# The product of C and the state in three parts, B and C loaded by chunk, and another order in layer 1

## The chip, the cores and the metric

The kernel runs on one core of one Trainium2 chip. The metric is the device time of one execution in microseconds. Three runs of the kernel before took 1805.58, 1814.24 and 1804.48 us; the median is 1805.58 us. TensorE (PE) multiplies, VectorE (DVE), ScalarE (ACT) and GpSimd (POOL) do the elementwise work, and SyncE (SP) issues most transfers. PEld in the profile is TensorE's weight load.

## The reference

Two layers over 1024 latent and 256 context tokens of width 1024, all in float32. Layer 0 has a gated linear recurrence beside a differential attention; the change doesn't touch it. Layer 1 is a Mamba-2 mixer in both directions, with 32 heads of 64 in 4 groups that share B and C. It is computed in chunks of 128 tokens:

```python
z, xbc, dt = jnp.split(u @ w_in, [SSD_INNER, SSD_INNER + SSD_CONV_DIM], axis=-1)
xbc = jax.nn.silu(dwconv_centred(xbc, conv_w, conv_b))
xs, Bm, Cm = jnp.split(xbc, ...)
...
CB = jnp.einsum("bclgn,bcsgn->bcgls", Cc, Bc)
y_diag = jnp.einsum("bcgls,bgrcls,bcsgrp->bclgrp", CB, Lmat, Xc)
states = jnp.einsum("bclgn,bgrcl,bclgrp->bcgrpn", Bc, decay_states, Xc)
...
y_off = jnp.einsum("bclgn,bcgrpn,bgrcl->bclgrp", Cc, states_in, jnp.exp(A_cs))
...
y = ys[0] + ys[1] + d_skip * xs          # both directions
y = rms_norm(y * silu(z), norm_w) @ w_out  # norm per group, then the output projection
```

The product `Cc` with `states_in` in `y_off` is the one that the change computes in another way.

## The kernel before, in words

Layer 1 runs from about 830 to 1812 us of the profile. It has four stages.

- The dt stage (`dt_block`, 830 to 911 us) makes the step sizes and their sums, and turns three tables (`wd`, `ea`, `dtt`) with TensorE transposes. It stores `d_acs`, `d_ncs` and `d_et` in HBM.
- The blocks of B, C and x (`conv_block`, 911 to 1240 us). Each group has one block of B, one of C and four of x. A block is a projection of 128 columns over all tokens (L303, from `proj`), four convolution taps on DVE (L329, L331) and an activation on ACT (L712). A projection is made as three float32r products: weight and input are each split in a high part and a rest, and high x high, rest x high and high x rest are summed. ACT casts the high part of the weights (L282), DVE subtracts for the rest (L283). The x blocks are then transposed to token order (L723), scaled on POOL (L744, `x2w`), split (L752 on ACT, L753 on POOL) and stored in `d_x`. B is split likewise (`bkh`, `bkl`) and stored in `d_bk`; B and C also go to `d_bt` and `d_ct`, whole.
- The z blocks (`z_block`, 16 of them; nz, which is 3, come before the B and C blocks, the rest at 1240 to 1410 us). Between them go the first steps of the states of group 0: `k.step` takes x2 from `d_x` (L908) and `bk` (L887) and multiplies them (L929).
- The chunk stage (`ssd`, 1410 to 1812 us): 4 groups of 8 chunks. `front(s)` makes the masks (L1050, L1052, L1053, L1055), CB (L1034) and the product of C with the states of both directions (L1061, one float32 matmul each), which DVE and POOL scale and add (L1064, L1067, L1069). `mid(s)` transposes that sum into psdy (L1078), adds the product within the chunk (L1083), and gates and splits it. `back(s)` is the output projection (L1119) and the sum over groups in `acc` (L1129); in the last group it also makes the final norm (L1134, L1143). `front` runs two steps ahead of `back`, `mid` one. `r_g` and `r_y` are the reciprocal roots that the two norms need, made on POOL (L218).

Inside each engine instructions run in order. A scheduler writes that order from its own model of the program when the kernel is built, so a line that is moved in the source moves in the engines' rows as far as the scheduler lets it. Pools are regions of on-chip memory: a pool that is opened where another was closed waits for what was using the space.

## Time and profile before

| what | us |
|---|---|
| median of three runs | 1805.58 |
| the profiled execution | 1813.9 |
| its span (first to last instruction) | 1812.1 |
| TensorE busy in the span | 1728.8 (95%) |
| VectorE busy | 1130.6 (62%) |
| ScalarE busy | 820.4 (45%) |
| GpSimd busy | 484.8 (27%) |

The chain of work that ended last is 71% TensorE, 9% DVE, 6% DMA, 5% POOL, 4% ACT. So the kernel is mostly as long as its matmuls, and the rest is in places where TensorE stands. The granted clock of TensorE (PEclk) is a share of its full speed; 0.50 is the lower of its two levels.

How to read rows of the trace: a row of the timeline has a start, a length, the engine, the line, the operation and what it writes and reads; in brackets is the idle time before it and what ended it. xN at the end means N instructions in a row. Matmuls are pipelined: a row's length has overlap with its neighbours in it, so the distance of two starts tells what a matmul takes.

### The profile page before, as it was taken

Reading aid. Unit: us, or ns where it says so; the run is one execution under the profiler, and the core shown is the slowest. Engines: PE = TensorE matmul, PEld = TensorE weight load, DVE = VectorE, ACT = ScalarE, POOL = GpSimd, SP = SyncE. Lnnn points to the kernel's source line nnn. Section 1 sums busy time; section 2 is a strip of 40 time slices with the busy share of each in tenths; the row PEclk is TensorE's granted clock in tenths of the full one; section 3 lists DMA queues with packets and bytes.
Section 4 is the critical chain, followed back from the end, with each engine's and each line's share of the span. In section 5 each row is a group of like instructions: output and inputs, shape, how many; then the busy total and the mean of one; then the engine's idle time right before and its main releaser. Section 6 shows DMA issues by size and latency. Waiting matters only on the chain.

```text
span 1812.1 us, 24291 instructions
## 1 busy us (share of the span) xinstructions
PE 1728.8 (95%) x8946; PEld 1343.8 (74%) x8946; DVE 1130.6 (62%) x1646; ACT 820.4 (45%) x1607; POOL 484.8 (27%) x459
## 2 busy tenths in 40 slices
PE   5999999999999998999999999998899899999997
PEld 2765478888888877886778888887678577777775
DVE  4635566766748476666666666665121667878787
ACT  5552464565536465544344443435111555434443
POOL 1200210000000000110029494948010344444432
PEclk8999999999999999999899999999899999999999
DMA  8336532622231224433238584858843677777764
GB/s 270 121 96 191 156 105 94 168 60 76 79 108 65 71 94 148 135 124 92 68 122 217 166 225 152 227 161 242 286 148 102 205 247 270 252 258 252 248 229 146
DMA packets 264637, 293.45 MB, mean 162 GB/s; under 512 B 16393, under 2 KB 213006, under 8 KB 264006
## 3 DMA queue, kind: packets, MB, share of 16 engines
q1 hardware_dynamic: 236336, 262.73, 46.3%
q10 hardware_dynamic: 28182, 29.16, 4.9%
q8 instruction: 71, 1.16, 0.3%
q14 instruction: 48, 0.39, 0.1%
HBM read 187.49 MB, written 100.42 MB: 159 GB/s over the span
## 4 chain that ended last, share of the span: by engine, by line
PE 71%; DVE 9%; DMA 6%; POOL 5%; ACT 4%; issue 4%; ACTq 0%; SPq 0%; DVEq 0%; POOLq 0%
PE psap L303 19%; PE pscp L303 10%; PE psap L1119 7%; PE psbp L303 7%; PE pscp L1427 3%; PE psat L591 3%; PE psat L929 2%; PE psdo L1061 2%; PE psap L1427 2%; PE scores L539 2%; PE psat L587 1%; PE scores L540 1%; PE psdy L1083 1%; POOL x2w L744 1%; DMA wm<-in_w_mod_dram 1%
## 5 line engine op out<-in xcount | busy, mean ns | idle before, releaser
L331 DVE SCALAR_TENSOR_TENSOR xbc<-xp_xb,pb,xbc 128x1283 f32<-128x1283 f32 (+1 forms) x72 | 141.7, 1972 | 2.9
L744 POOL TENSOR_TENSOR x2w<-tok_x,wd 128x1152 f32<-128x1152 f32 (+2 forms) x48 | 118.2, 2488 | 47.3 <-ACT tok_x L724 47.3
L940 POOL TENSOR_TENSOR s<-s,etb 128x512 f32<-128x512 f32 x64 | 70.9, 1107 | 205.0 <-DVE s L941 96.7
L602 POOL TENSOR_TENSOR ors<-z,mhalf 128x4 f32<-128x4 f32 (+1 forms) x12 | 14.5, 1212 | 380.4 <-DVE z L600 313.8
L941 DVE TENSOR_TENSOR s<-s,psat 128x512 f32<-128x512 f32 x64 | 43.6, 681 | 100.0 <-PE psat L929 76.5
L753 POOL TENSOR_TENSOR x2l<-x2w,x2h 128x1152 fp32r<-128x1152 f32 x32 | 104.4, 3282 | 0.1
L1119 PE MATMUL psap<-wo1h,yh 128*128 128x512 f32 x256 | 102.4, 400 | 0.0
L1119 PE MATMUL psap<-wo1h,yl 128*128 128x512 f32 x256 | 100.9, 395 | 1.5 <-DVE yl L1090 1.5
L1119 PE MATMUL psap<-wo1l,yh 128*128 128x512 f32 x256 | 101.1, 395 | 0.0
L329 DVE TENSOR_SCALAR xbc<-xp_xb,pb 128x1283 f32<-128x1283 f32 (+1 forms) x24 | 31.1, 1294 | 108.2 <-ACT xp_xb L321 86.3
L303 PE MATMUL pscp<-u1H,wh_xb 128*128 128x512 f32 x232 | 93.5, 403 | 0.0
L303 PE MATMUL pscp<-u1H,wl_xb 128*128 128x512 f32 x232 | 93.3, 402 | 0.0
L303 PE MATMUL pscp<-u1L,wh_xb 128*128 128x512 f32 x232 | 93.2, 402 | 0.0
L303 PE MATMUL psap<-u1H,wl_z 128*128 128x512 f32 x224 | 89.3, 399 | 0.0
L303 PE MATMUL psap<-u1H,wh_z 128*128 128x512 f32 x224 | 89.2, 398 | 0.0
L303 PE MATMUL psap<-u1L,wh_z 128*128 128x512 f32 x224 | 89.1, 398 | 0.0
L564 ACT ACTIVATE p<-scores,nm 128x1024 f32<-128x1024 f32 x64 | 71.5, 1118 | 28.4 <-DVE nm L563 20.8
L929 PE MATMUL psat<-x,bk 128*128 128x512 f32 x216 | 75.5, 457 | 7.8 <-DMA x<-d_x 7.8
L539 PE MATMUL scores<-kk,xq 128*128 128x512 f32 (+1 forms) x208 | 77.2, 383 | 3.7 <-ACT p L564 2.7
L752 ACT CAST x2h<-x2w 128x1152 fp32r<-128x1152 f32 x32 | 37.2, 1161 | 88.1 <-POOL x2w L744 88.1
L540 PE MATMUL scores<-kk,xl 128*128 128x512 f32 (+1 forms) x208 | 72.7, 361 | 0.0
L591 PE MATMUL psat<-v,wT 128*128 128x128 f32 x572 | 71.3, 278 | 0.0
(479 smaller groups left out, 5083.1 us busy)
## 6 DMA issues: line engine op xcount, KB each, us to landing
...
```

Of the source, the lines that this page charges most:

```text
L303: nc.tensor.matmul(ps[:n, :w_], l[:, k, :], r[:, k, t0 : t0 + w_], start=(k == 0 and i == 0), stop=(k == KT - 1 and i == 2))
L331: nc.vector.scalar_tensor_tensor(out[:, j0 : j0 + n], xp[:, j0 + k : j0 + k + n], cw(k), out[:, j0 : j0 + n], OP.mult, OP.add)
L539: nc.tensor.matmul(out, xq[m][:, qs], kk[m][:, k0 : k0 + n], start=True, stop=False)
L540: nc.tensor.matmul(out, xl[:, m, qs], kk[m][:, k0 : k0 + n], start=False, stop=True)
L564: nc.scalar.activation(pr[m][:, NCTX:], scores[m], AF.Exp, bias=nm[:, m : m + 1], accum_out=zz[:, 1, m : m + 1])
L591: nc.tensor.matmul(po[:, :P], wT[:, j, :], v[:, j, :], start=(j == 0), stop=(j == nkt - 1))
L744: nc.gpsimd.tensor_tensor(x2[:, o : o + n, :].rearrange("p c (h e) -> p c h e", e=64), t[:, a0:a1, :].rearrange("p c (h e) -> p c h e", e=64),
L753: nc.gpsimd.tensor_tensor(l, x2, h.bitcast(F32), OP.subtract)
L929: nc.tensor.matmul(ps, bk[:, l, t, :], x2[:, r, :], start=(i == 0), stop=(i == 2))
L940: nc.gpsimd.tensor_tensor(sn, self.prev[g, d], self.et[:, hs, t : t + 1].to_broadcast([P, 8, 64]), OP.mult)
L1119: nc.tensor.matmul(po, l[:, q, :], w[:, n], start=(q == 0 and i == 0), stop=(q == 3 and i == 2))
L1427: nc.tensor.matmul(ps, l[:, k, :], r[:, k, n], start=(k == 0 and i == 0), stop=(k == KT - 1 and i == 2))
```

## The change

Part (a), the order of layer 1: the pool p1 is opened before the dt stage's own pool instead of after it, and a new pool p1s holds the split tiles; the transposes of the three tables are put in a function `turn`, called after z block 0; z block 3 is computed before the last x block is finished (before, only its weights were fetched there); the group's loads and the first two x2 loads come before z block 4. The transfers of `et` go from ACT's queue to SP's. Part (b): C and each state are split in a high part and a rest, and C times the state is three float32r products. C's parts are made once for each group and stored in `d_cs`, the state's parts are made by `state_parts`, with ACT's cast and POOL's subtraction, in tiles of one buffer. Part (c): B and C in float32, and C's parts, are stored by chunk and loaded by chunk. Part (d): the multiplication `yg` of the last group is on POOL, but for the last chunk. The tiles `cb` and `td` have one buffer instead of two.

```diff
-    nc.scalar.dma_start(dr["et"], tot)
+    nc.sync.dma_start(dr["et"], tot)
...
+    def turn():
+        for src, dst in ((rm, wd), (acs, ea), (dt, dtt)):
+            for j0, n in ((0, 8), (8, 2)):
+                ps = c.psum()
+                for j in range(n):
+                    nc.tensor.transpose(ps[:, j * 64 : (j + 1) * 64], src[:, (j0 + j) * P : (j0 + j + 1) * P], c.ident[:64, :64])
+                pv = ps[:, : n * 64].rearrange("p (j h) -> p j h", h=64)
+                if dst is dtt:
+                    o = 2 if j0 == 0 else 0
+                    nc.vector.tensor_copy(dtt[:, j0 + o - 2 : j0 + n - 2, :], pv[:, o:n, 32:64])
+                else:
+                    nc.vector.tensor_copy(dst[:, j0 : j0 + n, :], pv)
+
+    return (wd, ea, et, dtt), turn
...
+        pool = s1.enter_context(tc.tile_pool(name="p1", bufs=2, side="right"))
         with tc.tile_pool(name="dtp", bufs=1, side="right") as dp:
-            tabs = dt_block(c, a, xdt, dp, scst, dr)
-        pool = s1.enter_context(tc.tile_pool(name="p1", bufs=2, side="right"))
-        for i in range(nz):
+            tabs, turn = dt_block(c, a, xdt, dp, scst, dr)
+            z_block(c, a, 0, uH, uL, zp, dr)
+            turn()
+        spool = s1.enter_context(tc.tile_pool(name="p1s", bufs=2, side="right"))
...
+        def by_chunk(e, dst, src):
+            e.dma_start(dst.rearrange("c p l -> p c l"), src.rearrange("p (c l) -> p c l", l=P))
...
-                nc.scalar.dma_start(dr["ct"][g], xc[:, 259:XC])
+                by_chunk(nc.scalar, dr["bc"][g, :, :, 1, :], xc[:, 259:XC])
+                h, l = (spool.tile([P, NLAT], F32R, name=f"ct{m}{g}", tag=f"ct{m}", bufs=1) for m in "hl")
+                nc.scalar.copy(h, xc[:, 259:XC])
+                nc.gpsimd.tensor_tensor(l, xc[:, 259:XC], h.bitcast(F32), OP.subtract)
+                store.append(lambda: [by_chunk(nc.sync, dr["cs"][g, :, :, m, :], x.bitcast(F32)) for m, x in enumerate((h, l))])
...
-        prefetch(c, a["o_w_in"][0][:, nz * P : (nz + 1) * P], f"z{nz}")
+        z_block(c, a, nz, uH, uL, zp, dr)
...
-    for i in range(nz, 16):
+    k.group(0)
+    for n in range(2):
+        k.step_x(0, "p", n)
+    for i in range(nz + 1, 16):
         z_block(c, a, i, uH, uL, zp, dr)
         if i == EARLY:
             early, rest = ssd(c, a, k, dr, S, out, h_d)
             early()
-        if i == nz:
-            k.group(0)
-            k.load_bc(0)
-            for n in range(3):
-                k.step_x(0, "p", n) if n < 2 else None
-        else:
-            n = i - nz - 1
-            if n < 9:
-                k.step(0, "p", n)
-                if n + 2 < 9:
-                    k.step_x(0, "p", n + 2)
-            if n >= 9 or n in (6, 7):
-                k.step(0, "j", {6: 0, 7: 1, 9: 2}.get(n, 2)) if n in (6, 7, 9) else None
+        n = i - nz - 2
+        if 0 <= n < 9:
+            k.step(0, "p", n)
+            if n + 2 < 9:
+                k.step_x(0, "p", n + 2)
+        if n in (6, 7, 9):
+            k.step(0, "j", {6: 0, 7: 1, 9: 2}[n])
...
+    def state_parts(s):
+        g, it = divmod(s, NCH)
+        ch = chunk_of(g, it)
+        out = []
+        for d in range(2):
+            st = k.st[g, d, ch].rearrange("p h e -> p (h e)")
+            h, l = (p1.tile([P, 512], F32R, name=f"s{m}{g}_{ch}{d}", tag=f"s{m}{d}", bufs=1) for m in "hl")
+            nc.scalar.copy(h, st)
+            nc.gpsimd.tensor_tensor(l, st, h.bitcast(F32), OP.subtract)
+            out.append((h, l))
+        sts[s] = out
...
+        bc = p1.tile([P, 2, P], F32, name=f"bc{nm}", tag="bc")
+        nc.sync.dma_start(bc, dr["bc"][g, ch])
+        cs = p1.tile([P, 2, P], F32R, name=f"cs{nm}", tag="cs")
+        nc.sync.dma_start(cs.bitcast(F32), dr["cs"][g, ch])
...
-        cb = p1.tile([P, 1, P], F32, name=f"cb{nm}", tag="cb")
+        nc.tensor.matmul(pcb[:, :P], bc[:, 0, :], bc[:, 1, :], start=True, stop=True)
+        cb = p1.tile([P, 1, P], F32, name=f"cb{nm}", tag="cb", bufs=1)
...
-            nc.tensor.matmul(py, ct[:, l0 : l0 + P], k.st[g, d, ch].rearrange("p h e -> p (h e)"), start=True, stop=True)
+            sh, sl = sts[s][d]
+            for i, (l, r) in enumerate(((0, sh), (1, sh), (0, sl))):
+                nc.tensor.matmul(py, cs[:, l, :], r, start=(i == 0), stop=(i == 2))
...
-                nc.vector.tensor_tensor(y, acc[:, n], gp[:, n], OP.mult)
+                e = nc.vector if s == N - 1 else nc.gpsimd
+                e.tensor_tensor(y, acc[:, n], gp[:, n], OP.mult)
...
+            if 2 <= s + 2 < N:
+                state_parts(s + 2)
```

TensorE in a chunk of the first groups, around the product of C (`ct` or `cs`) with a state (`s`, or its parts `sh` and `sl`) into `psdo`; before:

```order
L1034 MATMUL psda_12280<-ct_10543,bt_10541 128x128
L1050 MATMUL psda_12298<-At_10463,Rt_10466 128x512
L1061 MATMUL psdo_12314<-s_10683,ct_10543 128x512
L1050 MATMUL psda_12300<-At_10463,Rt_10466 128x512
L1061 MATMUL psdo_12318<-s_12058,ct_10543 128x512
L929 MATMUL psat_12324<-x_12247,bk_11540 128x512 x3
L1119 MATMUL psap_12345<-wo1h_11518,yh_2_12131 128x512
L1119 MATMUL psap_12345<-wo1l_11519,yh_2_12131 128x512
L1050 MATMUL psda_12306<-At_10463,Rt_10466 128x512
```

and of the change:

```order
L1049 MATMUL psda_12575<-bc_0_12569 128x128
L1065 MATMUL psda_12593<-At_10540,Rt_10543 128x512
L931 MATMUL psat_12636<-x_12532,bk_12526 128x512
L1065 MATMUL psda_12595<-At_10540,Rt_10543 128x512
L1078 MATMUL psdo_12609<-sh_00_12534,cs_0_12571 128x512 x2
L1078 MATMUL psdo_12609<-sl_00_12535,cs_0_12571 128x512
L1078 MATMUL psdo_12615<-sh_01_12538,cs_0_12571 128x512 x2
L1078 MATMUL psdo_12615<-sl_01_12539,cs_0_12571 128x512
L1128 MATMUL psat_12644<-ones,sr_1_12409 128x2
L1136 MATMUL psap_12650<-wo1h_11589,yh_1_12402 128x512
L1065 MATMUL psda_12601<-At_10540,Rt_10543 128x512
```

Each L1061 has become three L1078, high C with the high state, the rest of C with it (x2 stands for both), and high C with the state's rest; what stands around them is the same work, with a row of the state's step drawn between the masks.

POOL in the last group, two chunks; before:

```order
L218 TENSOR_TENSOR r_g_1_15015<-v_g_1_15013,mhalf 128x1
L218 TENSOR_TENSOR r_y_1_15057<-v_y_1_15055,mhalf 128x1
L1093 TENSOR_TENSOR sq_3_15083<-sq_3_15083 128x256
L1067 TENSOR_TENSOR td_4_15103<-td_4_15103,to_40_15130 128x512
L940 TENSOR_TENSOR s_15280<-s_15142,etb 128x512
L1095 TENSOR_TENSOR sr_3_15086<-sq_3_15083 128x128
L218 TENSOR_TENSOR r_g_2_15153<-v_g_2_15151,mhalf 128x1
L218 TENSOR_TENSOR r_y_2_15195<-v_y_2_15193,mhalf 128x1
```

and of the change:

```order
L1027 TENSOR_TENSOR sl_50_15677<-s_15461,sh_50_15676 128x512
L1084 TENSOR_TENSOR td_4_15572<-td_4_15572,to_40_15601 128x512
L1152 TENSOR_TENSOR yg_20_15658<-acc_2_15618,gp_0_11567 128x512
L1152 TENSOR_TENSOR yg_21_15663<-acc_2_15618,gp_0_11567 128x512
L1027 TENSOR_TENSOR sl_51_15681<-s_14130,sh_51_15680 128x512
L218 TENSOR_TENSOR r_y_2_15668<-v_y_2_15666,mhalf 128x1
L218 TENSOR_TENSOR r_g_3_15780<-v_g_3_15778,mhalf 128x1
L1027 TENSOR_TENSOR sl_60_15829<-s_15615,sh_60_15828 128x512
L1110 TENSOR_TENSOR sq_4_15702<-sq_4_15702 128x256
L1112 TENSOR_TENSOR sr_4_15705<-sq_4_15702 128x128
```

The two subtractions `sl` and the two `yg` of another chunk stand between `td`, `r_y` and `r_g`, which were alone there with `sq`, `sr` and the state's scaling.

SP where the states of group 0 begin, after the last stores of x2; before:

```order
L758 DMA d_x_7295<-x2h_10428 128x9x128
L758 DMA d_x_7295<-x2l_10429 128x9x128
L279 DMA wst_z_10759<-in_o_w_in_dram 128x8x128
L887 DMA bk_10539<-d_bk 128x2560
L894 DMA bt_10541<-d_bt 128x1024
L894 DMA ct_10543<-d_ct 128x1024
L908 DMA x_10545<-d_x_7295 128x1024
```

and of the change:

```order
L279 DMA wst_z_10771<-in_o_w_in_dram 128x8x128
L761 DMA d_x_7295<-x2h_10505 128x9x128
L761 DMA d_x_7295<-x2l_10506 128x9x128
L761 DMA d_x_7295<-x2h_10510 128x9x128
L761 DMA d_x_7295<-x2l_10511 128x9x128
L897 DMA bk_10564<-d_bk 128x2560
L910 DMA x_10566<-d_x_7295 128x1024
```

The two whole loads `bt` and `ct` between `bk` and the first `x` are gone, and the next weights of z stand ahead of the last stores.

TensorE where the x block 0 ends and x block 1 begins; before:

```order
L303 MATMUL pscp_7867<-u1L,wh_xb_7811 128x512
L303 MATMUL pscp_7909<-u1Hc,wh_xb_7905 128x256
L303 MATMUL pscp_7909<-u1Hc,wl_xb_7906 128x256
L303 MATMUL pscp_7909<-u1Lc,wh_xb_7905 128x256
L303 MATMUL pscp_7909<-u1Hc,wh_xb_7905 128x256
```

and of the change:

```order
L303 MATMUL pscp_7874<-u1L,wh_xb_7818 128x512
L303 MATMUL pscp_7916<-u1Hc,wh_xb_7912 128x256
L303 MATMUL pscp_7942<-u1H,wh_xb_7912 128x512
L303 MATMUL psap_7968<-u1H,wh_xb_7912 128x512
L303 MATMUL psap_8045<-u1Hc,wh_xb_8041 128x256
L303 MATMUL pscp_8071<-u1H,wh_xb_8041 128x512
L303 MATMUL pscp_7916<-u1Hc,wl_xb_7913 128x256
L303 MATMUL pscp_7916<-u1Lc,wh_xb_7912 128x256
```

The first products of five sums, of this block and of the one after it (8041), now stand ahead of this block's second product.

## Rows read from the trace of the kernel before

**Rows 1.** Stretches: length, busy of PE, PEld, DVE, ACT, POOL; clock; DMA share; GB/s.
```profile
911.00:1240.00 329.00, 326.96 (x1703) 272.82 (x1703) 215.79 (x115) 145.58 (x204) 215.07 (x148) 1.00 0.64 185
1240.00:1300.00 60.00, 48.29 (x201) 38.31 (x202) 16.64 (x9) 17.17 (x24) 27.54 (x12) 0.91 0.91 275
...
1410.00:1440.00 30.00, 22.60 (x98) 13.17 (x97) 22.48 (x38) 17.27 (x42) 10.26 (x10) 0.89 0.67 228
1440.00:1700.00 260.00, 258.71 (x1357) 190.42 (x1357) 195.23 (x360) 118.28 (x307) 112.92 (x130) 1.00 0.75 256
1700.00:1780.00 80.00, 79.02 (x422) 57.90 (x420) 70.22 (x141) 39.59 (x111) 28.72 (x37) 1.00 0.66 220
```

**Rows 2.** Timeline of TensorE in one chunk.
```profile
1519.88 1.02 PE L1061 MATMUL psdo<-s,ct 128*128 128x512 f32 x2
1520.34 0.80 PE L1050 MATMUL psda<-At,Rt 128*128 128x512 f32 x1
1520.98 1.02 PE L1061 MATMUL psdo<-s,ct 128*128 128x512 f32 x2
1521.43 1.25 PE L929 MATMUL psat<-x,bk 128*128 128x512 f32 x3
1522.53 0.39 PE L1119 MATMUL psap<-wo1h,yh 128*128 128x512 f32 x1
1522.76 0.40 PE L1119 MATMUL psap<-wo1l,yh 128*128 128x512 f32 x1
```

**Rows 3.** Groups by line: count, busy us, mean ns, idle before and its releasers.
```profile
L753 POOL TENSOR_TENSOR x2l<-x2w,x2h 128x1152 fp32r<-128x1152 f32 x32 | 104.4, 3282 | 0.1
...
L1061 PE MATMUL psdo<-s,ct 128*128 128x512 f32 x128 | 66.5, 601 | 0.4 <-DVE to L1069 0.3
...
L283 DVE TENSOR_TENSOR wl_xb<-wst_xb,wh_xb 128x1024 fp32r<-128x1024 f32 x24 | 54.4, 2266 | 14.7 <-ACT wh_xb L282 14.7
...
L1067 POOL TENSOR_TENSOR td<-td,to 128x512 f32<-128x512 f32 x32 | 41.3, 1291 | 39.7 <-ACT td L1044 39.7
...
L1069 DVE TENSOR_TENSOR to<-psdo,td 128x512 f32<-128x512 f32 x32 | 22.1, 691 | 16.7 <-POOL td L1067 16.7
...
L1089 ACT CAST yh<-psdy 128x512 fp32r<-128x512 f32 x32 | 18.7, 585 | 12.9 <-DVE psdy L1086 11.7
...
L1134 DVE TENSOR_TENSOR yg<-acc,gp 128x512 f32<-128x512 f32 x16 | 10.5, 684 | 0.1
```

**Rows 4.** Timeline of TensorE, waits at the z blocks.
```profile
1252.38 1.09 PE L723 MATMUL pscu<-ident,xbc 128*128 128x128 f32 x8 [3.57 <-ACT xbc L712]
...
1285.91 1.62 PE L929 MATMUL psat<-x,bk 128*128 128x512 f32 x3 [7.23 <-DMA x<-d_x]
```

**Rows 5.** Stretch behind the second of these waits; columns as in Rows 1.
```profile
1285.00:1290.00 5.00, 4.09 (x10) 3.25 (x11) 0.00 (x0) 2.12 (x3) 1.06 (x1) 0.50 0.62 211
```

**Rows 6.** Timeline of SP's queue: the loads for group 0.
```profile
1274.59 0.33 SPq L887 DMA_DIRECT2D bk<-d_bk  x1
...
1275.91 14.95 SPq L908 DMA_DIRECT2D x<-d_x  x5
```

**Rows 7.** Timeline of all engines at the end of the dt stage.
```profile
908.10 1.04 ACT L282 CAST wh_xb<-wst_xb 128x1024 fp32r<-128x1024 f32 x1 [8.99 <-PE pscp L303]
909.18 1.23 DVE L283 TENSOR_TENSOR wl_xb<-wst_xb,wh_xb 128x1024 fp32r<-128x1024 f32 x1 [8.55 <-ACT wh_xb L282]
...
910.62 0.86 ACT L321 COPY xp_xb<-psap 128x256 f32<-128x256 f32 x2 [1.47 <-DMA d_ncs<-hl]
910.92 0.10 POOL L315 MEMSET xp_xb<- 128x2 f32 x1 [53.70 <-DMA d_ncs<-hl]
...
911.04 0.39 PE L303 MATMUL psap<-u1Hc,wh_xb 128*128 128x256 f32 x1 [2.98 <-ACT xp_xb L321]
```

**Rows 8.** Timeline of TensorE, the last two waits.
```profile
1778.64 0.66 PE L1078 MATMUL psdy<-ident,to 128*128 128x128 f32 x4 [0.43 <-DVE v_g L216]
...
1789.55 0.76 PE L1078 MATMUL psdy<-ident,to 128*128 128x128 f32 x4 [2.03 <-DVE v_g L216]
```

More of the change, by code (lines that the diff above doesn't have):

```diff
@@ L687, in dt_block @@
     et = cst.tile([P, 64, NT], F32, name="etb")
-    nc.scalar.dma_start(et, dr["et"].rearrange("h c -> (h c)").unsqueeze(0).to_broadcast([P, 64 * NT]).rearrange("p (h c) -> p h c", c=NT))
-    for src, dst in ((rm, wd), (acs, ea), (dt, dtt)):
-        for j0, n in ((0, 8), (8, 2)):
-            ps = c.psum()
-            for j in range(n):
-                nc.tensor.transpose(ps[:, j * 64 : (j + 1) * 64], src[:, (j0 + j) * P : (j0 + j + 1) * P], c.ident[:64, :64])
-            pv = ps[:, : n * 64].rearrange("p (j h) -> p j h", h=64)
-            if dst is dtt:
-                o = 2 if j0 == 0 else 0
-                nc.vector.tensor_copy(dtt[:, j0 + o - 2 : j0 + n - 2, :], pv[:, o:n, 32:64])
-            else:
-                nc.vector.tensor_copy(dst[:, j0 : j0 + n, :], pv)
-    return wd, ea, et, dtt
+    nc.sync.dma_start(et, dr["et"].rearrange("h c -> (h c)").unsqueeze(0).to_broadcast([P, 64 * NT]).rearrange("p (h c) -> p h c", c=NT))
+    def turn():
[11 more added lines that the diff above has]
+    return (wd, ea, et, dtt), turn
 def conv_block(c, a, i, uH, uL, pool, slices, then=None):
@@ L782, in layer1 @@
         "et": dram.tile([64, NT], F32, name="d_et"),
-        "bt": dram.tile([G, P, NLAT], F32, name="d_bt"),
-        "ct": dram.tile([G, P, NLAT], F32, name="d_ct"),
+        "bc": dram.tile([G, NCH, P, 2, P], F32, name="d_bc"),
+        "cs": dram.tile([G, NCH, P, 2, P], F32, name="d_cs"),
         "bk": dram.tile([G, P, 2, NT, P], F32, name="d_bk"),
@@ L797, in layer1 @@
         c.wcyc = 0
+        pool = s1.enter_context(tc.tile_pool(name="p1", bufs=2, side="right"))
         with tc.tile_pool(name="dtp", bufs=1, side="right") as dp:
-            tabs = dt_block(c, a, xdt, dp, scst, dr)
-        pool = s1.enter_context(tc.tile_pool(name="p1", bufs=2, side="right"))
-        for i in range(nz):
+            tabs, turn = dt_block(c, a, xdt, dp, scst, dr)
+            z_block(c, a, 0, uH, uL, zp, dr)
+            turn()
+        spool = s1.enter_context(tc.tile_pool(name="p1s", bufs=2, side="right"))
+        for i in range(1, nz):
             z_block(c, a, i, uH, uL, zp, dr)
         late, store, splits = [None], [], []
+        def by_chunk(e, dst, src):
+            e.dma_start(dst.rearrange("c p l -> p c l"), src.rearrange("p (c l) -> p c l", l=P))
         def block(i, slices, done):
@@ L812, in done_b @@
             def done_b(xb, g=g):
-                nc.scalar.dma_start(dr["bt"][g], xb[:, 259:XC])
+                by_chunk(nc.scalar, dr["bc"][g, :, :, 0, :], xb[:, 259:XC])
                 def tok():
                     t = tok_major(c, xb, pool, f"b{g}")
-                    h = pool.tile([P, NT, P], F32R, name=f"bkh{g}", tag="bkh", bufs=1)
-                    l = pool.tile([P, NT, P], F32R, name=f"bkl{g}", tag="bkl", bufs=1)
+                    h = spool.tile([P, NT, P], F32R, name=f"bkh{g}", tag="bkh", bufs=1)
+                    l = spool.tile([P, NT, P], F32R, name=f"bkl{g}", tag="bkl", bufs=1)
                     def split():
@@ L837, in tok @@
                             store.pop()()
-                        for l, f in zip((splits, store), x_states(c, t, 4 * g + q, pool, tabs[0], dr)):
+                        for l, f in zip((splits, store), x_states(c, t, 4 * g + q, spool, tabs[0], dr)):
                             l.append(f)
@@ L888, in group @@
         self.bk[g] = bk
-    def load_bc(self, g):
-        pair = []
-        for nm in ("bt", "ct"):
-            t = (self.xpool if g % 2 else self.bcp).tile([P, NLAT], F32, name=f"{nm}{g}", tag=f"{nm}{g % 2}", bufs=1)
-            self.c.nc.sync.dma_start(t, self.dr[nm][g])
-            pair.append(t)
-        self.bcs[g] = pair
     def load_x(self, g, t):
@@ L1002, in ssd @@
     maskb = k.mask.bitcast(U32).to_broadcast([P, 4, P])
-    bcs, load_bc = k.bcs, k.load_bc
     wos = {}
@@ L1017, in chunk_of @@
         return NCH - 1 - it if g % 2 == 0 else it
+    sts = {}
+    def state_parts(s):
[9 more added lines that the diff above has]
+        sts[s] = out
     def front(s):
@@ L1022, in front @@
         q = s % 2
-        bt, ct = bcs[g]
         nm = f"{g}_{ch}"
@@ L1041, in front @@
         nc.vector.scalar_tensor_tensor(cf, dtt[:, ch, 8 * g : 8 * g + 8], cd, k.dbc[:, 8 * g : 8 * g + 8], OP.mult, OP.add)
-        td = p1.tile([P, 8, 64], F32, name=f"td{nm}", tag="td")
+        td = p1.tile([P, 8, 64], F32, name=f"td{nm}", tag="td", bufs=1)
         for h in range(8):
@@ L1159, in early @@
         for s in range(2):
+            state_parts(s)
             fr[s] = front(s)
@@ L1177, in rest @@
                     k.group(g + 1)
-                    load_bc(g + 1)
                 if s < 0:
```

6 lines of the change are left out of this document (removed).

## Prediction

> **What bounds the kernel now.** I read the busy time by stretch first. In the chunk stage proper TensorE is busy 258.71 of 260 us and then 79.02 of 80 us, at full granted clock, while POOL is busy 112.92 and 28.72 us [rows 1]: a matmul less is a matmul's time less there, as long as nobody makes TensorE wait. Around it lie two seams where TensorE stands: 48.29 busy of 60 us at 1240 to 1300 and 22.60 of 30 at 1410 to 1440, with clocks of 0.91 and 0.89. Then I read TensorE's own row order inside a chunk for the price of a matmul [rows 2], the groups by line for the other engines' prices [rows 3], and the seams one wait at a time [rows 4 to 8].
>
> **C times the state.** Before, each of 64 such products is one f32 matmul, shown as two records at L1061. Starts give its real price, since a record's length includes queueing. From 1519.88 to 1522.53 stand two f32 pairs, one L1050 and three L929, 2.65 us [rows 2]. A float32r 128x512 matmul starts 0.23 us after the one before it (1522.53 to 1522.76, both L1119), so four of them take 0.92 and a pair (2.65 - 0.92)/2 = 0.865 us. Three float32r products take 3 x 0.23 = 0.69. Saved: 64 x 0.175 = 11.2 us, all on the engine that sets the end. That three in a row with three weight loads keep 0.23 is not shown for this tile, but L929 is the same pattern and fits the sum; bounds 64 x 0.09 = 6 us (if each product costs 0.26) to 64 x 0.23 = 14.7.
> A row and a page differ here. By the Trainium skill (FP8 and Floating Point Precision, TensorE Precision Notes) true FP32 makes four passes through the array; at 0.23 us a pass that is 0.92, and the estimate by the page would be 64 x 0.23 = 14.7 us. The trace has 0.865, or 3.8 passes, and I keep to the trace.
>
> **The price of the parts.** Each chunk gets two ACT casts and two POOL subtractions of 128x512 (L1026, L1027). The cast of yh of that size takes 0.585 us [rows 3], so ACT gets 1.2 us a chunk. POOL's float32r subtraction takes 3.282 us for 1152 columns [rows 3], or 1.46 for 512: 2.9 us a chunk. A chunk lasts 12.4 us in groups 0 to 2 (260 us for 21 chunks), so POOL goes from 43% to some 67% busy [rows 1]. The parts are asked for a whole step ahead of their product and the states two steps ahead, which is the cover. If it is gone, it comes through td: POOL's L1067 stands behind L1027 in the new order, DVE's L1069 waits for it already, 16.7 us over 32 [rows 3], and the transposes into psdy are behind that on TensorE. Least 0; most 32 x 2.9 = 93 us, if POOL's new work were wholly in the chain. I take +2 us, near the least, since the waits of DVE for POOL today leave TensorE 99.5% busy. The same split once per group on the whole of C (ACT 1.04 us for 1024 columns [rows 7], POOL 2.9) stands in the x blocks, where POOL is busy 215.07 of 329 us and TensorE never waits [rows 1]: 4 x 2.9 = 11.6 us on POOL, hidden, 0 on the end; bounds 0 to 11.6.
>
> **B and C by chunk.** Two loads of 512 KB per group go, 256 KB per chunk come: bc and cs. That is 1 MB a group more over 99 us, at 256 GB/s mean [rows 1] 4 us of transfer beside a DMA share of 0.75. Each load is issued a step ahead of use: 0 (0 to +3, if loads run late). The stores by chunk are issued on ACT's and SP's queues between other work: 0.
>
> **The seam at 1240 to 1300.** Three things lie there. TensorE waits 3.57 us for the last x block's activation before its transposes [rows 4]; then 7.23 us for the first x2 (L929 by DMA x); and after that the clock is at the lower of its two levels for at least 1285 to 1290 [rows 5]. SP issues bk at 1274.59 and x after it at 1275.91, with bt and ct (1 MB) between them, and all land about 1285.9 [rows 6, 4]. The new order puts z3's matmuls ahead of the last transposes: 13 at 0.23 us cover 3.0 of the 3.57. It takes out bt and ct: 1 MB at 275 GB/s [rows 1] is 3.8 us of the 7.23. Against that, the three us of matmuls drawn forward are missing later as cover for x, which still has to wait for the last x2 stores, so what is certain is the shorter load. I take -5 us (3.8, and a little over 1 for the clock); bounds -13 (3.57 + 7.23 + 2.5 for five microseconds at half clock) and +1 (all hidden by the stores in front).
>
> **The dt stage and block x1.** TensorE waits 2.98 us at 911.04 for the copies of xp, which wait for a memset on POOL that waits for the d_ncs store, because p1 lies where the dt pool lay [rows 7]. With p1 opened earlier this wait goes: -3. But the new TensorE order draws five first matmuls of blocks x1 and x2 ahead of x1's own second product, and they need wh casts that now stand on ACT behind bkh and cth. Before, the cast was done at 909.1, long ahead, and the low part 1.23 us later [rows 7]. Behind a cast of 1280 columns (1.3 at 1.04 per 1024), one of 1.04 and a copy, with 1.2 for the low part, less five matmuls of 0.23, I get +3 once. Sum 0 (-3 to +3). The turn of wd, ea and dtt stays at its place in TensorE's order: 0. The et transfer moves from ACT's queue to SP's, and its reader is 300 us later: 0.
>
> **The seam at 1410 to 1440.** Of 7.4 us idle [rows 1] part is waits for e and cb, which stay. The next group's bt and ct (1 MB) go, and a chain psdo, sh, sl, psdo through single buffers comes. 0 (-4 to +4).
>
> **yg to POOL.** 14 of 16 instructions of 0.684 us leave DVE [rows 3], which in the last group is busy 70.22 of 80 us [rows 1]. TensorE waits 2.03 us near the end for DVE [rows 8]. Freed: 1.3 us in front of that wait, and a little more clock: -2. POOL pays some 1.3 us for each (L1067 has 1.291 [rows 3]). A chunk of the last group lasts 10.9 us (1778.64 to 1789.55 [rows 8]) and has 3.9 us of POOL now (28.72 in 80 [rows 1]); with the parts and yg that is 3.9 + 2.9 + 2.6 = 9.4, in order, and r_g stands behind yg there. Bounds -4 to +6.
> A rule that speaks against it: the low part of a weight block (128x1024) takes DVE 1.23 us with POOL idle [rows 7] and 2.27 us on average over all 24 blocks, most of them beside a busy POOL [rows 3]. By the Trainium skill (GPSIMD Engine Reference, Key points) GpSimd shares its SBUF interfaces with VectorE and contends with those DVE instructions that have two SBUF inputs, and the trace agrees in these two numbers. By it only L1143 in the last group would grow, 16 times by at most 0.6 us, 10 us on DVE and not on TensorE; DVE's freed 9.6 us would pay for it, and the -2 would become 0. The rest of DVE in a chunk reads one operand from PSUM (e, to, yl at 0.68 to 0.69), and I see no growth in it.
>
> **Sum.** -11.2 + 2 - 5 + 0 + 0 - 2 = -16.2 us. The profiled execution took 1813.9 us (span 1812.1), so 1797.7 by its own time. It lies 8.3 us above the median of the runs, 1805.6; 16.2 off the median is 1789.4, which I predict.
>
> **Rivals.** (1) Only the product's saving arrives: the seams and the tail keep their length because x2's stores and the dependent chains set them, and 2 to 4 us of the saving go into waits. -8, 1798. For it: the 7.23 us are released by x, not by bt. Against: 1 MB sat between the two on one queue. (2) Slower: POOL sets the chunk. Every td comes one L1027 later (1.46 us) with no cover, 32 x 1.46 = 47 us against -18.2 (the sum without its +2): +28.5, about 1834. It eats the gain from 0.57 us of TensorE wait per chunk, and is slower than the bound from 0.85. For it: POOL at 67%, then 86% in the last group, running in order, with DVE already waiting for it. Against: a step of 12 us lies between the parts and their reader. (3) More: the 1 MB less and the filled wait take most of both seams and their slow clock. The first is worth up to 13, the second some 7.4 and 0.11 x 30 = 3 of clock; if half of what I left on the table comes, -26, about 1779. (4) The product isn't cheaper, since three weight loads show where two did (a load takes 0.19 us of 0.23): only the small terms are left and cancel, 1805. Against: L1119 runs at 0.23 with a load each.
>
> **How the numbers follow.** Chances: forecast 0.56, rival 1 0.14, rival 2 0.09, rival 3 0.16, rival 4 0.05. What this kernel can tell from no change is some 0.5%, 9.0 us: faster is under 1796.5, slower over 1814.6. Faster: 0.56 + 0.16 = 0.72. Same: rivals 1 and 4, 0.19. Slower: rival 2, 0.09. The likeliest case by itself runs from 1783 to 1796. The range reaches from 1775 (rival 3 with the bounds of its terms) to 1804, and leaves out most of rivals 2 and 4 and the far end of 3.
>
> **What would show it.** Right: L1078 starts 0.23 us apart, three per product; chunks of some 12.0 us; TensorE at 99% busy from 1440 on; the wait for x near 1280 under 4 us; no wait at 911. Wrong: DVE L1069 waiting for POOL's L1084 for over 1 us a chunk and TensorE under 97% there; r_g waited for by acc in the last group; a wait of over 4 us in block x1; TensorE standing as long as before for x.

## The result, and the profile after

The changed kernel is slower. Its median is 1857.82 us (1849.63 to 1859.75, 4 runs), against 1808.66 us of the kernel before on the same chip; the ratio is 1.0248, 95% interval [1.0219, 1.0277]. The forecast was 1789.4 and the range ended at 1804. The profiled execution has a span of 1854.7 us against 1812.1.

The stretches of the changed kernel that answer to [rows 1], in the same columns:

```profile
1240.00:1300.00 60.00, 51.67 (x221) 40.82 (x220) 15.93 (x11) 20.18 (x29) 26.59 (x12) 0.94 0.94 293
...
1410.00:1440.00 30.00, 24.41 (x114) 16.23 (x113) 26.40 (x39) 20.77 (x48) 21.09 (x18) 0.89 0.69 233
1440.00:1700.00 260.00, 242.22 (x1246) 176.00 (x1244) 181.21 (x319) 126.45 (x315) 148.12 (x154) 0.98 0.69 237
1700.00:1780.00 80.00, 73.78 (x383) 52.37 (x381) 63.19 (x109) 39.52 (x103) 47.17 (x50) 1.00 0.66 224
```

The loss is in the chunk stage. TensorE was busy 258.71 of its 260 us from 1440 and is now busy 242.22, with 1246 matmuls done there instead of 1357, though a product of C now counts three and not two. POOL has more to do, 148.12 us for 112.92. From the first td to the last (L1067, now L1084) the stage took 373.4 us (1414.0 to 1787.4) and takes 419.6 (1411.8 to 1831.4): 46.2 us more. The span grew by 42.6, since the first td is 2.2 us earlier and what follows the last one 1.4 us shorter. Summed over 2-us stretches, TensorE stands 37.3 us there instead of 9.7, and 6.6 us more go to the lower clock. The other 12 of the 46.2 us lie in rows in which TensorE counts as busy; what makes these longer is not shown.

The groups of the changed kernel from 1400 us on, in the columns of [rows 3]:

```profile
L1027 POOL TENSOR_TENSOR sl<-s,sh 128x512 fp32r<-128x512 f32 x62 | 81.2, 1324 | 30.3 <-ACT sh L1026 27.7 <-PE psdo L1078 2.4
...
L1026 ACT CAST sh<-s 128x512 fp32r<-128x512 f32 x62 | 36.7, 612 | 12.5 <-PE psdo L1078 10.5 <-POOL sl L1027 1.5 <-DVE s L943 0.5
...
L1086 DVE TENSOR_TENSOR to<-psdo,td 128x512 f32<-128x512 f32 x32 | 22.0, 689 | 10.0 <-POOL td L1084 9.0
L1152 POOL TENSOR_TENSOR yg<-acc,gp 128x512 f32<-128x512 f32 x14 | 18.1, 1305 | 6.6 <-DVE acc L1146 6.6
```

The prices of the new instructions are those of the prediction: 1.32 us for a subtraction (1.46 forecast), 0.61 for a cast (0.585), 1.31 for yg on POOL (1.3). The wait of DVE for td even fell, from 16.7 us [rows 3] to 9.0. So the prices were foreseen, and what they would hold up was not. What TensorE waits for, over the whole span (engine, what it was to write, who released it: us in all, times, longest):

```profile
PE psap L1136 <- DVE acc L1146: 9.7, 11, 1.7
...
PE psda L1065 <- DVE e L1070: 5.8, 8, 2.1
...
PE psdy L1100 <- DVE e L1070: 5.3, 3, 1.9
```

A chain that ends in such a wait stands in one of the long chunks. All engines of the changed kernel, as start, length, engine, line, operation and, in brackets, the idle time before:

```profile
1551.25 1.29 POOL L1084 TENSOR_TENSOR td<-td,to 128x512 f32<-128x512 f32 x1 [2.21 <-DVE psdo L1081]
...
1552.95 2.55 POOL L1027 TENSOR_TENSOR sl<-s,sh 128x512 fp32r<-128x512 f32 x2
...
1554.06 0.15 DVE L216 TENSOR_SCALAR v_g<-psat 128x1 f32<-128x1 f32 x1
...
1555.59 1.06 POOL L942 TENSOR_TENSOR s<-s,etb 128x512 f32<-128x512 f32 x1
...
1556.60 0.55 POOL L218 TENSOR_TENSOR r_g<-v_g,mhalf 128x1 f32<-128x1 f32 x1
1557.19 0.75 DVE L1146 SCALAR_TENSOR_TENSOR acc<-psap,r_g,acc 128x512 f32<-128x512 f32 x1 [2.97 <-POOL r_g L218]
1557.85 0.68 DVE L1070 TENSOR_TENSOR e<-psda,cb 128x512 f32<-128x512 f32 x1
...
1558.59 0.73 PE L1100 MATMUL psdy<-e,xk 128*64 128x128 f32 x8 [1.85 <-DVE e L1070]
```

v_g is ready at 1554.21, but POOL is in the two subtractions till 1555.5 and then scales a state, so r_g starts at 1556.60. DVE, in order, stands 2.97 us in front of acc with e behind it, and TensorE stands 1.85 us for e. Before, POOL had no subtractions to do there.

Over the whole stage this chain is small. DVE's group for acc and what ended its idle time, in the kernel before, the changed kernel and e1, which leaves the subtractions out:

```profile
L1129 DVE SCALAR_TENSOR_TENSOR acc<-psap,r_g,acc 128x512 f32<-128x512 f32 x48 | 34.9, 747 | 18.3 <-POOL r_g L218 15.4 <-PE psap L1119 2.7
...
L1146 DVE SCALAR_TENSOR_TENSOR acc<-psap,r_g,acc 128x512 f32<-128x512 f32 x48 | 35.1, 744 | 8.7 <-POOL r_g L218 7.0 <-PE psap L1136 0.8 <-DMA hres<-d_h 0.7
...
L1145 DVE SCALAR_TENSOR_TENSOR acc<-psap,r_g,acc 128x512 f32<-128x512 f32 x48 | 34.9, 743 | 3.6 <-POOL r_g L218 2.5 <-PE psap L1135 1.1
```

DVE stood 15.4 us for r_g before, in 17 short waits, and stands 7.0 in the changed kernel, in four, of which the 2.97 above is the longest. TensorE's wait for acc, 9.7 us, hardly falls without the subtractions (e1) and not without any parts (e8):

```profile
PE psap L1135 <- DVE acc L1145: 8.6, 9, 2.0
...
PE psap L1138 <- DVE acc L1148: 9.8, 11, 2.4
```

So it is not the subtractions' doing. It is gone where bc and cs are loaded on ACT's queue (e14, e19), and where TensorE's order is forced (e10, e12), with other waits in its place. What falls from the changed kernel to e1 are TensorE's waits for e, from 11.1 to 5.7 us in the stage, for `to`, from 4.7 to 2.6, and for the state s, from 5.0 to 3.5.

A second thing stands on SP's queue. The same rows for SP, where the loads of the next chunk are issued:

```profile
1545.90 0.32 SPq L1155 DMA_DIRECT2D d_acc<-acc  x1
...
1548.08 0.63 SPq L1039 DMA_DIRECT2D At<-d_acs  x1
1548.77 0.57 SPq L1040 DMA_DIRECT2D Rt<-d_ncs  x1
1549.38 0.59 SPq L1042 DMA_DIRECT2D zc<-d_z  x1
1559.22 0.33 SPq L1155 DMA_DIRECT2D d_acc<-acc  x1
1559.59 0.43 SPq L1044 DMA_DIRECT2D bc<-d_bc  x1
1560.06 0.79 SPq L1046 DMA_DIRECT2D cs<-d_cs  x1
```

At, Rt and zc of a chunk are issued by 1550; then the store of acc waits on the queue for DVE until 1559.22, and bc and cs of the same chunk come behind it. bc is the operand of that chunk's first matmul (L1049). In the kernel before, B and C were loaded once for a group; the same store stood on SP then too, ahead of loads of Rt and zc.

The other waits that the prediction named, on TensorE of the changed kernel:

```profile
926.18 0.38 PE L303 MATMUL pscp<-u1Hc,wh_xb 128*128 128x256 f32 x1 [1.62 <-ACT wh_xb L282]
...
1254.41 1.09 PE L726 MATMUL pscu<-ident,xbc 128*128 128x128 f32 x8 [0.54 <-ACT xbc L715]
...
1284.74 1.62 PE L931 MATMUL psat<-x,bk 128*128 128x512 f32 x3 [6.40 <-issue]
```

The 2.98 us at 911 [rows 7] are gone; block x1 costs 1.62 instead. The 3.57 us [rows 4] are 0.54. The 7.23 us for x [rows 4] are still 6.40, for which the profile names no releaser. With bt and ct gone, x is used 7.2 us after its issue and not 10.0; but it is issued 1.65 us later, at 1277.56 against 1275.91 [rows 6].

### The profile page after: what moved, and what is told of

Its sections match the earlier page's. It is cut to its first block, busy times and chain, and to the rows that moved or that the text cites. A ratio compares the mean times of both kernels' runs of the same rounds, so it can differ in the third digit from the quotient of the medians.

```text
span 1854.7 us, 24714 instructions
## 1 busy us (share of the span) xinstructions
PE 1747.0 (94%) x9010; PEld 1355.2 (73%) x9010; DVE 1140.5 (61%) x1632; ACT 858.4 (46%) x1675; POOL 592.6 (32%) x541
## 4 chain that ended last, share of the span: by engine, by line
PE 68%; DVE 11%; POOL 6%; ACT 5%; issue 5%; DMA 4%; ACTq 0%; SPq 0%; POOLq 0%; DVEq 0%
PE psap L303 20%; PE pscp L303 10%; PE psbp L303 7%; PE psap L1136 5%; PE pscp L1445 3%; PE psat L591 3%; PE psap L1445 2%; PE psat L931 2%; PE scores L539 2%; PE scores L540 1%; PE psat L587 1%; PE psdy L1100 1%; POOL x2w L747 1%; PE psda L1065 1%; DMA wm<-in_w_mod_dram 1%
## 5 line engine op out<-in xcount | busy, mean ns | idle before, releaser
L1136 PE MATMUL psap<-wo1h,yh 128*128 128x512 f32 x256 | 105.4, 414 | 9.7 <-DVE acc L1146 9.7
L1136 PE MATMUL psap<-wo1l,yh 128*128 128x512 f32 x256 | 103.2, 403 | 1.1 <-DVE wo1l L1011 1.1
L1136 PE MATMUL psap<-wo1h,yl 128*128 128x512 f32 x256 | 102.3, 400 | 0.2 <-DVE yl L1107 0.2
L1027 POOL TENSOR_TENSOR sl<-s,sh 128x512 fp32r<-128x512 f32 x64 | 84.2, 1330 | 38.6 <-ACT sh L1026 36.0
L303 PE MATMUL psap<-u1H,wh_z 128*128 128x512 f32 x208 | 83.1, 399 | 0.0
L303 PE MATMUL psap<-u1H,wl_z 128*128 128x512 f32 x208 | 82.9, 399 | 0.0
L303 PE MATMUL psap<-u1L,wh_z 128*128 128x512 f32 x208 | 82.7, 398 | 0.0
L931 PE MATMUL psat<-x,bk 128*128 128x512 f32 x216 | 67.3, 416 | 10.7 <-issue 6.8
```

What stands on the lines that cost most here:

```text
L303: nc.tensor.matmul(ps[:n, :w_], l[:, k, :], r[:, k, t0 : t0 + w_], start=(k == 0 and i == 0), stop=(k == KT - 1 and i == 2))
L931: nc.tensor.matmul(ps, bk[:, l, t, :], x2[:, r, :], start=(i == 0), stop=(i == 2))
L1027: nc.gpsimd.tensor_tensor(l, st, h.bitcast(F32), OP.subtract)
L1136: nc.tensor.matmul(po, l[:, q, :], w[:, n], start=(q == 0 and i == 0), stop=(q == 3 and i == 2))
```

## The experiments

Medians, and ratios to the kernel before on the same chip (95% interval). The kernel before had medians from 1808.7 to 1815.2 us in these comparisons, so two runs are compared by their ratios where it matters:

| run | us | ratio |
|---|---|---|
| changed kernel | 1857.8 | 1.0248 [1.0219, 1.0277] |
| e1_no_sub | 1839.8 | 1.0147 [1.0117, 1.0177] |
| e2_sub_on_dve | 1846.8 | 1.0190 [1.0158, 1.0221] |
| e4_yg_on_dve | 1860.4 | 1.0267 [1.0235, 1.0298] |
| e5_f32_product | 1820.4 | 1.0041 [1.0022, 1.0061] |
| e6_no_sub_cb_td_2 | 1840.7 | 1.0144 [1.0129, 1.0159] |
| e7_no_sub_sh_2 | 1839.3 | 1.0136 [1.0121, 1.0152] |
| e8_no_parts | 1831.9 | 1.0097 [1.0074, 1.0121] |
| e9_f32_cb_td_2 | 1810.1 | 0.9990 [0.9965, 1.0015] |
| e10_order | 1855.1 | 1.0230 [1.0187, 1.0272] |
| e11_order_sub_dve | 1854.5 | 1.0240 [1.0212, 1.0269] |
| e12_order_no_parts | 1828.5 | 1.0092 [1.0064, 1.0121] |
| e13_order_f32 | 1819.3 | 1.0032 [1.0008, 1.0056] |
| e14_loads_on_act | 1833.3 | 1.0108 [1.0088, 1.0128] |
| e15_loads_on_act_sub_dve | 1827.7 | 1.0083 [1.0057, 1.0108] |
| e16_cs_once | 1831.6 | 1.0097 [1.0076, 1.0119] |
| e17_order_part_only | 1810.6 | 0.9974 [0.9948, 1.0000] |
| e18_product_alone | 1827.6 | 1.0073 [1.0033, 1.0113] |
| e19_loads_on_act_no_parts | 1808.3 | 0.9981 [0.9961, 1.0001] |

**The subtractions.**

```diff
...
-            nc.gpsimd.tensor_tensor(l, st, h.bitcast(F32), OP.subtract)
-            out.append((h, l))
+            out.append((h, h))
```

> POOL's 64 subtractions L1027 are left out: the third product of C with a state uses the high part again instead of the state's rest, so TensorE's and ACT's work is that of the changed kernel and the rest of the state is missing from the result. Theory 1 (a subtraction of 1.3 us, twice a chunk, stands on POOL in front of r_g and td; DVE's acc waits for r_g, DVE's e stands behind acc, and TensorE waits for e): the chunk stage falls from 419.6 to some 370 us, 1795 to 1812 in all. Rival A (the single-buffered parts and ACT's casts, 1.1 us a chunk): at most 5 us less than the changed kernel, over 1850. Rival B (the loads by chunk, or the order of the whole stage): over 1840.

1.0% less, 18 us: the subtractions are a part of the loss, and less than half. All three ranges are missed, rival B's by a hair. Theory 1 is far too large, and the path that it names, by r_g and acc, carries little of the 18 us, as the groups above show.

```diff
-            nc.gpsimd.tensor_tensor(l, st, h.bitcast(F32), OP.subtract)
+            nc.vector.tensor_tensor(l, st, h.bitcast(F32), OP.subtract)
```

> The subtractions L1027 are on DVE instead of POOL, nothing else. Theory 1: POOL is as free as before and DVE gets 2 x 0.68 us a chunk of 12, from 75% to 86% busy: 1800 to 1820. A rival by which any further work on the engines between two products costs its own time: DVE's 1.4 us for POOL's 2.6, so half of the loss stays, about 1835. Rivals A and B: over 1845.

0.6% less, with an interval that touches that of the changed kernel: far from theory 1, and in the range of rivals A and B. DVE's price was not the 0.68 us counted on: its subtraction takes 0.68 in the median, but 0.94 on average and 1.79 at most. The 22 of 64 that take over 0.8 us all run beside POOL's work, the longest beside td.

**yg, and the one float32 product.**

```diff
-                e = nc.vector if s == N - 1 else nc.gpsimd
+                e = nc.vector
```

> The multiplication yg is on DVE in all chunks, as before the change. Theory 1: POOL has 2.5 us a chunk less in the last group, whose chunks last 14 us against 11 to 12 before; 8 to 18 us less than the changed kernel, 1840 to 1850. If yg on POOL is not part of the loss: within 3 us of the changed kernel, 1855 to 1861, or up to 3 us more for DVE's 14 x 0.68 us.

No gain. yg on POOL is not part of the loss.

```diff
...
-            sh, sl = sts[s][d]
-            for i, (l, r) in enumerate(((0, sh), (1, sh), (0, sl))):
-                nc.tensor.matmul(py, cs[:, l, :], r, start=(i == 0), stop=(i == 2))
+            nc.tensor.matmul(py, bc[:, 1, :], k.st[g, d, ch].rearrange("p h e -> p (h e)"), start=True, stop=True)
```

> The product of C with a state is one float32 matmul again, so the parts of C and of the state, their stores and loads (cs) are gone; the order of the first stages, B and C loaded by chunk and yg on POOL stay. Theory 1: the cost of the parts goes and so do the 11 us that the three products give; the seams' gain of some 2 us and a little loss by yg stay: 1802 to 1818. Rival B (loads by chunk or the order are the cause): over 1835.

37 us less, a little over theory 1's range: nearly all of the loss comes with the three products, their parts and the loads of cs.

**Buffers.** In e6 `bufs=1` is left out for `cb` and `td`, on e1; in e7 `sh` has `bufs=2`, on e1.

> Without the 64 subtractions, as in e1_no_sub (the third product uses the high part again, so the rest of the state is missing from the result), and with two buffers for cb and td as before the change. e1_no_sub took 1839.8 us: the subtractions explain 18 of the 49 us. Theory 2 (with one buffer, the next chunk's cb and td can't be written before this chunk's last e and to are done, so its masks start late): 1812 to 1826. Rival A (ACT's casts of the state stand in front of td and the exponentials): within 5 us of 1840. Rival C (the scheduler's new order of TensorE's rows): within 5 us of 1840.

> Without the 64 subtractions, as in e1_no_sub (the rest of the state is missing from the result), and with two buffers for each sh, in the room that sl leaves. Rival A in the form that one buffer makes ACT cast right after the product before, ahead of td and the exponentials: 1820 to 1830. If the cast's time counts and not its buffer, or under theory 2 and rival C: 1835 to 1843.

Both stay with e1. Theory 2 and the buffer form of rival A fall where the subtractions are out and the loads stand on SP.

**No parts at all.** On e1, after the first chunk:

```diff
     def state_parts(s):
+        if s:
+            sts[s] = sts[0]
+            return
...
```

> No parts of the state are made after the first chunk: all three products of every chunk read the first chunk's high part, so the casts and the subtractions are out, the result is that of a wrong state, and TensorE's work is that of the changed kernel. If the casts and the subtractions are the whole loss (rival A and theory 1): 1795 to 1806, 11 under what the f32 product gave on its better runs (1810). Under theory 2 or rival C, which don't touch the casts: 1822 to 1840.

Another 0.5%, with intervals that just overlap, and 1.0% over the kernel before is left. The run takes out more than the casts: its products no longer wait for the state of their own chunk. The loss has a second cause that is neither cast nor subtraction.

> The product of C with a state is one float32 matmul as in e5_f32_product, and cb and td have two buffers. Theory 2: one buffer costs here too, 5 to 12 us less than the 1820 of e5_f32_product, so 1808 to 1815, level with the kernel before or under it. If one buffer costs only where the parts are in the way, or not at all: 1817 to 1823.

Level with the kernel before and 0.5% under e5, with intervals that do not overlap: in theory 2's range. With the f32 product the second buffers of cb and td are worth some 9 us. Whether they are with the three products, once the loads are off SP, no run shows.

**The order of TensorE.** In the kernel before, and in e5 up to the third group, each chunk runs mid, front, back on TensorE; in the changed kernel the scheduler mixes them. Edges of issue order put the cycle back; lp is the last L1136 of the chunk before, lx the last L1100 of mid, ld the last L1078 of front:

```diff
+                with behind(lp):
+                    md[s + 1] = mid(s + 1, *fr.pop(s + 1))
...
+                    with behind(lx):
+                        fr[s + 2] = front(s + 2)
...
+                with behind(ld):
+                    back(s, [wos[4 * g + q] for q in range(4)], *md.pop(s))
```

> The changed kernel with three edges of issue order on TensorE for each chunk: the transposes of a chunk come behind the last output projection of the chunk two before it, the next masks behind the products in the chunk, and the output projection behind the product of C with the state. That is the cycle in which the kernel before and e5_f32_product issue (mid, front, back), which the scheduler gave up where the product became three short ones. Nothing else changes. e8_no_parts has no parts at all and yet takes 1832, 28 more than its TensorE work. Theory 3 (that order is some 25 to 30 us of the loss; the subtractions are the other 18): 1822 to 1838. Rival D (the short products themselves, or the loads of cs, not the order): 1850 to 1865.

> The same edges of issue order, and the subtractions L1027 on DVE instead of POOL. If theory 3 and theory 1 both hold and their parts add: 10 less than e10_order, 1808 to 1826. If the order alone was what put the subtractions in the way: the same as e10_order within 4 us. If DVE has no room: 5 to 10 us more than e10_order.

> As e8_no_parts (no casts and subtractions of the state after the first chunk, so all products read one wrong state) with the same edges of issue order. Theory 3: the floor of the change, 1795 to 1808. Rival D: 1825 to 1836, as e8_no_parts.

> e5_f32_product (one f32 product, no parts; the other parts of the change kept) with the same edges of issue order. Its order follows the cycle nearly everywhere up to the third group and breaks it in the fourth, so theory 3 gives 3 to 10 us less than e5_f32_product: 1802 to 1815, at or below the kernel before. If the edges themselves cost (TensorE standing for a load that another row could have covered): over 1822.

Theory 3 falls: with and without parts the edges change nothing that can be told from the kernel without them (e11 is 8 us over e2, with intervals that overlap). TensorE's order by itself is not the second cause. e10 and e12 lie in the ranges of rival D, the short products or the loads of cs; e13 lies between its two ranges.

**SP's queue.**

```diff
-        nc.sync.dma_start(bc, dr["bc"][g, ch])
+        nc.scalar.dma_start(bc, dr["bc"][g, ch])
...
-        nc.sync.dma_start(cs.bitcast(F32), dr["cs"][g, ch])
+        nc.scalar.dma_start(cs.bitcast(F32), dr["cs"][g, ch])
```

> The changed kernel with the two loads by chunk, bc and cs, issued on ACT's queue instead of SP's; nothing else. Theory 4 (SP issues in order: the store of acc stands ahead of the next chunk's loads and waits for DVE, and bc is the first thing that TensorE needs; in e12_order_no_parts TensorE waits 0.53 us for bc and 1.22 for x right behind such a store): SP is as free as before, the scheduler's order becomes as even as before, and 20 to 30 us go: 1828 to 1840; what stays is the subtractions. Rival E (the short products by themselves): over 1850. Rival F (the bytes: 1 MB a group more): over 1850.

1.4% less, 25 us, by the queue of two loads alone, as theory 4 had it. SP and ACT in e14, the same part of the stage:

```profile
1546.06 0.32 SPq L1155 DMA_DIRECT2D d_acc<-acc  x1
...
1558.29 0.33 SPq L1155 DMA_DIRECT2D d_acc<-acc  x1
```
```profile
1545.22 0.33 ACTq L1044 DMA_DIRECT2D bc<-d_bc  x1
1551.85 0.33 ACTq L1046 DMA_DIRECT2D cs<-d_cs  x1
1558.41 0.33 ACTq L1044 DMA_DIRECT2D bc<-d_bc  x1
```

The store still stands on SP, and bc and cs no longer stand behind it. The bc of 1545.22 is read by its L1049 at 1570.30, 25 us later; in the changed kernel the bc of 1559.59 is read at 1565.17, after 5.6 us. The median over the 32 chunks is 25.7 us in e14 and 6.8 in the changed kernel. No byte less is moved, so rival F falls.

A late bc is not enough for the loss, though. e9 loads bc on SP too, behind the same store (1549.94, bc at 1551.79), a median of 8.6 us ahead of its use, and is level with the kernel before. It has the f32 product and no cs.

> As e14_loads_on_act, with the subtractions L1027 on DVE. If theories 1 and 4 add up: 1808 to 1822, about level with the kernel before. If subtractions were only in the way because of the uneven order: within 5 us of e14.

Another 6 us, with intervals that overlap: less than the 11 of e2, and outside both ranges.

```diff
...
+        if s == 0:
+            cso[0] = p1.tile([P, 2, P], F32R, name="cso", tag="cs", bufs=1)
+            nc.sync.dma_start(cso[0].bitcast(F32), dr["cs"][g, ch])
+        cs = cso[0]
```

> As e12_order_no_parts, and cs is loaded once in the whole stage instead of in every chunk, so that all chunks use the first chunk's parts of C and of the state (a wrong product); bc is still loaded by chunk. Theory 4: one load less a chunk on SP, 5 to 15 us less than e12_order_no_parts (1828), 1812 to 1823. Rival E: 1824 to 1832.

Theory 4 misses and rival E, the short products by themselves, has the range. One load less in the order of e12 gave nothing. Against e13, which has the same edges and the same loads of bc, and the f32 product, e16 takes 0.65% or 12 us more, with intervals that do not overlap.

> Part (a) of the change alone on the kernel before: pools, turn, z block 3, the group's loads before z block 4; C times the state is one f32 product, B and C are loaded whole, yg is on DVE, cb and td have two buffers. What the first stages give: the first td of e5_f32_product came 13 us earlier than before. 1795 to 1804, the kernel that beats both. If the gain is lost again in the chunk stage: 1805 to 1815.

Part (a) alone is 0.26%, some 5 us, under the kernel before, with an interval that ends at 1; the 1795 to 1804 did not come. It has the lowest ratio of the table, though it can't be told from the kernel before with certainty.

**What is left.**

```diff
-                nc.tensor.matmul(py, ct[:, l0 : l0 + P], k.st[g, d, ch].rearrange("p h e -> p (h e)"), start=True, stop=True)
+            bk = k.bk[g]
+            for i, (l, m) in enumerate(((0, 0), (1, 0), (0, 1))):
+                ld[0] = nc.tensor.matmul(py, bk[:, l, tt, :], bk[:, m, 4 * d : 4 * d + 4, :].rearrange("p t l -> p (t l)"), start=(i == 0), stop=(i == 2))
```

> e17_order_part_only (median 1811, profile 1813) with nothing but the product changed: three float32r matmuls of the same shapes on the split B that is in the chip anyway (bk) in place of C and the state, with the issue edges of e10; no parts, no loads by chunk, a wrong product. If the prediction's price is right (0.865 to 0.69 us a product): 9 to 12 us less than e17, 1798 to 1803. If the price was misread, since a mask product beside these takes 0.30 to 0.34 us and not 0.23: 2 to 5 us less, 1806 to 1811. Rival E (the short products cost by themselves): over 1815.

17 us over e17: both ranges for the product's price are missed, and rival E's is met. It does not give the product's price by itself, since its order carries the edges as well: TensorE stands 19.2 us from 1412 to 1772 (e17: 9.3) and loses 9.4 to the clock. But the edges cost nothing with the f32 product (e5 to e13). So under this order the three products cost 12 to 17 us (e16, e18) for a reason that no run shows.

> As e8_no_parts (casts and subtractions of the state out after the first chunk, so a wrong state), with bc and cs loaded on ACT's queue as in e14; no edges of order. If SP's queue and the parts are the two causes and together the whole loss: e18's time within 8 us, 1800 to 1815. If a third cause stays: 1820 to 1832, as e8_no_parts.

1808: both causes out, the loss is gone (e8 with the other queue), and with it rival E as a price that the short products have in every order. And yet the 11 us of the product don't show: 0.9981 against 0.9974 of e17 and 0.9990 of e9, which have the f32 product.

Why they don't, the rows of e19 say. TensorE in e19, from the first matmul of a front to the output projection:

```profile
1502.27 0.49 PE L1051 MATMUL psda<-bc 128*128 128x128 f32 x2
1502.52 0.48 PE L1067 MATMUL psda<-At,Rt 128*128 128x512 f32 x1
1502.83 0.39 PE L1080 MATMUL psdo<-sh,cs 128*128 128x512 f32 x1
1503.12 0.50 PE L1067 MATMUL psda<-At,Rt 128*128 128x512 f32 x1
1503.45 1.09 PE L1080 MATMUL psdo<-sh,cs 128*128 128x512 f32 x4
1504.40 0.49 PE L1067 MATMUL psda<-At,Rt 128*128 128x512 f32 x1
1504.74 0.40 PE L1080 MATMUL psdo<-sh,cs 128*128 128x512 f32 x1
1504.97 0.86 PE L931 MATMUL psat<-x,bk 128*128 128x512 f32 x3
1505.67 0.40 PE L1138 MATMUL psap<-wo1h,yh 128*128 128x512 f32 x1
```

and in the kernel before, the row ahead of those in [rows 2]:

```profile
1519.33 0.49 PE L1034 MATMUL psda<-ct,bt 128*128 128x128 f32 x2
```

Before, 1519.33 to 1522.53 are 3.20 us with two masks; in e19, 1502.27 to 1505.67 are 3.40 with three. A mask product beside these takes 0.31 to 0.34 us to the next start (1502.52, 1503.12, 1504.40), and 0.23 among output projections, as the third mask of that chunk before:

```profile
1522.99 0.40 PE L1050 MATMUL psda<-At,Rt 128*128 128x512 f32 x1
1523.22 0.40 PE L1119 MATMUL psap<-wo1h,yl 128*128 128x512 f32 x1
```

Without the third mask e19 has 3.06 to 3.17, so two products give 0.03 to 0.14 us a chunk and not 0.35: 1 to 4 us in all. The 3.20 stands, within 0.01, in all thirteen chunks from 1440 to 1600; 3.40 (3.39 to 3.41) in eight of thirteen of e19, and more in the rest, with waits in most of these.

## Why the prediction was wrong

- **The product, -11.2: mis-sized.** It was worked out by giving the mask between two f32 pairs 0.23 us, the distance that it has among other rows. Beside the product it has 0.31 to 0.34, so the f32 product was not 0.865 but some 0.82 us, and the masks drawn into the new row cost more there. Measured 1 to 4 us, in the order of e19. On this term rival 4 was right in effect, for another reason.
- **The parts, +2: the failed step.** The cover was taken to hide the parts. Measured without them (changed kernel to e8, by ratios 0.0151 of 1813): 27 us, 18 for the subtractions (e1) and the rest for the casts and what goes with them. The cover, a step between the parts and their product, does hold for the product: TensorE waits 0.2 us for sl in the whole stage. It does not hold for others behind the parts on the same in-order engines. The reader named, td, carried little of it: DVE waits 9.0 us for td, less than before, and 9.6 without the subtractions; TensorE's waits for `to`, behind it, are 4.7 us, against 0.6 before and 2.6 without them. One chunk shows the path by r_g, acc and e; over the stage it is small, and most of how the 18 us reach TensorE stays open. Rival 2 had the price of a subtraction and the kind of the mechanism, but at td.
- **B and C by chunk, 0: the second failed step.** I counted bytes and a step ahead, not what stands on SP's queue: the store of acc between the loads. The step of some 12 us was a median of 6.8. Measured twice, by ratios: 25 us with parts (changed kernel to e14), 21 without (e8 to e19, 0.0116 of 1813). Shown is that the queue of these two loads makes it, in kernels with the three products. How it reaches TensorE is only argued: TensorE hardly waits for bc itself (0.2 us in the changed kernel), and its waits for acc (9.7 us there, 9.8 in e8) are gone in e14 and e19. I take it that the scheduler wrote the front later because its loads are late. e9, with a late bc and no loss, e16 and e18 don't fit smoothly and stay open, and which of the two loads counts was not run.
- **The seams, -5 and 0:** the wait of 3.57 us fell as said and the one for x fell by 0.8 only, not to under 4. The x1 wait was 1.62 against 2.98 removed. The first td is 2 us earlier, and part (a) alone gives 5 (e17), which can't be told from nothing with certainty.
- **yg, -2:** with yg back on DVE (e4) the kernel takes 2.6 us more, within the noise. The term is of the right size and not shown.
- **Single buffers of cb and td:** the sum has no term for them. With the f32 product they cost some 9 us (e5 to e9).

That the parts and the queue make up the loss is shown by e19. That they add is shown by taking them out in either order: the parts give 27 us with the loads on SP and 23 with them on ACT (e14 to e19), the queue 25 and 21, which agrees within the noise.
